# Delta rule on one core: both heads of a pair taken through the doublings step by step, and the next pair prepared ahead of the recurrence

## The chip, the core and the metric

The kernel runs on one core of a Trainium2 chip. Its engines are TensorE (PE, matrix products and the weight loads before them, PEld), VectorE (DVE), ScalarE (ACT), GpSimd (POOL) and SyncE (SP, which issues most transfers). The metric is the device time of one execution in microseconds, as the median of several runs. Lower is better.

## What is computed

Two small networks follow each other on a sequence of 512 tokens with 1024 channels, all in float32. The first block mixes tokens with a gated delta rule (4 heads of 128) beside a retention layer (4 heads of 128), then has an MLP; the second has two layers with attention and an MLP each. The change lies in the mixer of the first block. Its delta rule works on chunks; the kernel takes chunks of 128 tokens, four for each head, where the reference has 64.

```python
    kb = kc * betac[..., None]
    m = jnp.where(strict, jnp.einsum('nbhik,nbhjk->nbhij', kb, kc) * decay, 0.0)
    t_mat = lax.linalg.triangular_solve(eye + m, jnp.broadcast_to(eye, m.shape),
                                        left_side=True, lower=True, unit_diagonal=True)
    u_base = jnp.einsum('nbhij,nbhjv->nbhiv', t_mat, vb)
    w_mat = jnp.einsum('nbhij,nbhjk->nbhik', t_mat, kb * jnp.exp(gcum)[..., None])
...
    def step(state, inp):
        u_b, w_c, qk_c, qd_c, kd_c, cd_c = inp
        u = u_b - jnp.einsum('bhck,bhkv->bhcv', w_c, state)
        o = jnp.einsum('bhck,bhkv->bhcv', qd_c, state) + jnp.einsum('bhij,bhjv->bhiv', qk_c, u)
        state = state * cd_c[..., None, None] + jnp.einsum('bhck,bhcv->bhkv', kd_c, u)
        return state, o
```

## The kernel before

Activations lie with channels on the 128 partitions and the 512 tokens along the free side. Every projection is made of split products: `mm3` adds three products (high weight with high input, high with low, low with high part) to one PSUM tile `ps_pj`, and a projection of 1024 channels is eight such triples, 24 products. Three `ps_pj` tiles exist and five other PSUM tiles (pool `pw`). Weights come in blocks of 1 MB through SP's queue in the order of `_plan`, and ACT (`hi`, L252) and DVE (`lo`, L253) split each block before use.

The mixer treats the delta heads in two pairs (heads 0 and 1, heads 2 and 3), in these stages:

- `gdn_proj` projects keys, queries and values and applies the short convolution.
- `stage_a(hh)` prepares one head: keys and queries are transposed (`ps_kt`), ACT sums their squares (L602), DVE turns them into reciprocal roots (`col_rsqrt`, L425 to L435: a chain of small operations) and `brk`, `kdc`; `brk` is spread over the partitions on PE (`ps_bc`), then come the decay (`ps_gr`, `E`), the gram products (`ps_gram`, giving `N` and `QE`), `kd` (L652) and `vb`. `N` goes to DRAM (`d1`).
- `stage_b1(hp)` inverts the 16x16 diagonal blocks of the pair's triangular matrices on DVE (L678, L680) and sends them through DRAM to `cmp`.
- `stage_b2(hp)` lays them out as `T` and its transpose `U` (POOL, L696) and doubles the size of the inverted blocks three times. Each doubling has a product `ps_X` from `N` and `T`, its evacuation to `X` (DVE L721, ACT L744, ACT L764) and products `ps_T` and `ps_U`, which go back into `T` and `U`. The first doubling works on 128x64 pieces, the second on 32x32 blocks of the array, the third on 64x64 blocks. In each doubling head 0 goes through all its steps, then head 1.
- `stage_c(hp)` is the recurrence over the four chunks: for each chunk and head `ps_ks`, `vb` (DVE), `ps_u`, `u` (ACT, L790), `ps_S`, the state `S` (DVE) and `ps_o`.

Beside these stand projections of the retention heads (`rot_proj`, `ret_v`), their attention (`ret_attn`) and the gates (`gate`, with `finish`, which transposes the outputs and splits them into `mix`). Then `out_proj` applies the output weights.

A scheduler sets the order on each engine from the order of the code, dependencies and its own estimate of durations, and it fills PE's waits with products of projections. Three things in the code steer it: `in_order(i1, i2)` puts i2 behind i1, `early(prio)` gives a stretch an earlier priority, and the order of the calls at the end of `mixer`:

```python
        with early(p0):
            stage_b2(0, None, M_["rk1"])
            stage_c(0)
        with early(p1):
            stage_a(2)
            stage_a(3)
```

Only the first X product of a pair is bound to a place among the projections (`after_pe`).

Of the kernel before, what the change touches and what calls it, by code (L numbers as in the profile page):

```python
# [35 lines left out]

V_ATTN, V_MLP, V_FIN, V_MIX, V_MLP2, V_FIN2, V_GDNW, V_SUBLN, V_CONV = 0, 8, 16, 24, 40, 56, 64, 65, 66
# [20 lines left out]
def _plan():  # L58
# [6 lines left out]
    for c0, perm in ((2568, True), (2056, True), (3080, False), (1536, False), (3592, False)):  # L65
        out += [_w_cols("w_in", 0, c0 + hp * 256, perm) for hp in range(2)]
# [104 lines left out]
def build(nc, tc, a, out, phases=("mix", "mlp1", "A", "mlpA", "B", "mlpB")):  # L171
# [232 lines left out]
    def project(pieces, x, n=T, cols=P):  # L404
# [5 lines left out]
        for k in range(nk):  # L410
            hi, lo = pieces[k // KD]
            M_["pe"] = mm3(ps, (hi[:, k % KD, 0:cols], lo[:, k % KD, 0:cols]), x[k], k == 0, k == nk - 1)
# [52 lines left out]
    def out_proj(nk, x, scale_row, on_tile, reload=None, on_half=None):  # L465


        for m in range(KD):
# [20 lines left out]
            ps = project(pieces, x)  # L489
# [10 lines left out]
    def mixer(st):  # L500
# [88 lines left out]
        HD = [dict() for _ in range(4)]  # L589

        def stage_a(hh):
            H = HD[hh]
            kT, KQ, vT = H["kT"], H["KQ"], H["vT"]

            ssq = sp.tile([P, 8], F32, tag="ssq", name="ssq")
            for o, src in ((0, kT), (4, KQ[:, 1, :])):
# [6 lines left out]
                if o == 0:  # L603
                    ps_k = ps
# [7 lines left out]
            V.tensor_tensor(out=kdc, in0=rk, in1=GT["dkd"][:, :, hh], op=ALU.mult)  # L612

# [25 lines left out]
            for c2 in range(2):  # L639
# [6 lines left out]
                for aa, (o_, m_) in enumerate(((N, E2), (QE, E))):  # L646
# [4 lines left out]
            t = unit("L", NL, "kd")  # L651
            V.tensor_tensor(out=t.rearrange("p (c d) -> p c d", c=4), in0=ps_k.rearrange("p (c d) -> p c d", c=4),  # L652
                            in1=kdc.unsqueeze(2).to_broadcast([P, 4, P]), op=ALU.mult)
            H["kd"] = t
# [34 lines left out]
        def stage_b2(hp, after_g, after_pe):  # L689
# [19 lines left out]

            for i in range(2):  # L710
                H = HD[2 * hp + i]
                N, Tt, U = H["N"], H["T"], H["U"]
                X = unit("X", 2, "X")
                G.memset(X, 0.0)
# [6 lines left out]
                V.tensor_tensor(out=cols_of(X, 0).rearrange("p (c b) s -> p c b s", c=4),  # L721
                                in0=blocks(psx).rearrange("p (c b) s -> p c b s", c=4),
                                in1=cols_of(lm16, 0).unsqueeze(1).to_broadcast([P, 4, 4, 16]), op=ALU.mult)
                pst = pwt("ps_T", [P, 256])
                for c in range(4):
                    cs = slice(c * P, (c + 1) * P)
                    mm(blocks(pst[:, c * 64:c * 64 + 64]), U[:, cs], cols_of(X[:, cs], 0))
                V.tensor_tensor(out=cols_of(Tt, 0), in0=blocks(pst), in1=cols_of(Tt, 0), op=ALU.add)
                psu = pwt("ps_U", [P, 256])
                for c in range(4):  # L730
                    cs = slice(c * P, (c + 1) * P)
                    mm(blocks(psu[:, c * 64:c * 64 + 64]), X[:, cs], cols_of(U[:, cs], 1))
                V.tensor_tensor(out=cols_of(U, 1), in0=blocks(psu), in1=cols_of(U, 1), op=ALU.add)

            for i in range(2):
                H = HD[2 * hp + i]
                N, Tt, U = (H[k].rearrange("p (c i) -> p c i", c=4) for k in ("N", "T", "U"))
                ev, od = [slice(64 * b, 64 * b + 32) for b in range(2)], [slice(64 * b + 32, 64 * b + 64) for b in range(2)]
                psx = pwt("ps_X", [P, P])
                X = unit("X", 2, "X")[:, 0:P]  # L740
                for b in range(2):
                    for c in range(4):
                        mm(psx[od[b], c * 32:c * 32 + 32], N[ev[b], c, od[b]], Tt[ev[b], c, ev[b]])
                    act(out=X[od[b], :], in_=psx[od[b], :], func=AF.Copy)  # L744
                pst = pwt("ps_T", [P, P])
                psu = pwt("ps_U", [P, P])
                for b in range(2):
                    for c in range(4):
                        cs = slice(c * 32, c * 32 + 32)
                        mm(pst[od[b], cs], U[od[b], c, od[b]], X[od[b], cs])  # L750
                        mm(psu[ev[b], cs], X[od[b], cs], U[od[b], c, od[b]])
# [891 lines left out]
```

## Time and profile before

| | us |
|---|---|
| median of 3 runs | 1917.7 |
| lowest and highest run | 1908.59, 1922.01 |
| the profiled execution | 1922.43 |
| its span, first to last instruction | 1920.6 |

The profile is one execution. PE's share of busy time is high throughout, so what is worth reading is the granted clock (part 2 of the page, row PEclk), the few waits of PE, and the stretch of the mixer, which lasts from about 20 to 350 us of the span. The costliest groups of the page are the split products:

```profile
L189 PE MATMUL ps_pj<-xh,hi 128*128 128x512 f32 x1504 | 595.3, 396 | 2.1 <-ACT hi L277 2.1
```

A row of such a group has line, engine, operation, output and inputs, shape and count, then busy time, mean nanoseconds of one, and the idle time before them with what ended it. A product here is recorded with its length from issue to the last result; its cost is the distance between the starts of two neighbours. An ordinary float32 product is recorded as two instructions, so four products give eight records.

### The profile page before, as it was taken

The page shows a single profiled execution, that of the slowest core. Times are in us where ns is not written, and L with a number is a line of the kernel's source. Part 1 is how long each engine was busy: PE and PEld are TensorE (multiplying, and loading weights), DVE is VectorE, ACT ScalarE, POOL GpSimd, SP SyncE. Part 2 cuts the span into 40 slices and gives each one's busy share as a digit, 9 for nine tenths or more (in the row PEclk, how much of TensorE's full clock was granted, in tenths as well). Part 3 has the DMA queues.
Part 4 walks back from the last instruction along what each step waited for, and adds up shares of the span by engine and source line. Part 5 has one row for each costly group of instructions (what it writes and reads, how often), then busy time and mean ns, then how long its engine had stood idle before and what let it go on. Part 6 is the DMA issues. An engine that isn't in the chain of part 4 may idle for free.

```text
span 1920.6 us, 23573 instructions
## 1 busy us (share of the span) xinstructions
PE 1892.9 (99%) x9235; PEld 1554.4 (81%) x9235; DVE 1109.8 (58%) x2115; ACT 766.3 (40%) x1356; POOL 141.0 (7%) x133
## 2 busy tenths in 40 slices
PE   8999999999999999999999999999999999999998
PEld 6887777788888888877888888888888888888887
DVE  7795747666446676558543344447877754334433
ACT  5523324344234354345433134336656543213322
POOL 0231210011001103000000000001111000000000
PEclk9998989999999999999999999999999999999999
DMA  5231103222232234122323222333222232222321
GB/s 191 79 116 56 68 29 115 100 88 94 83 111 109 69 122 149 67 77 91 113 88 110 88 102 96 108 129 141 95 73 100 78 115 88 92 105 88 110 88 44
DMA packets 40271, 185.55 MB, mean 97 GB/s; under 512 B 9231, under 2 KB 11279, under 8 KB 22624
## 3 DMA queue, kind: packets, MB, share of 16 engines
q1 hardware_dynamic: 38416, 178.43, 26.5%
q0 software_dynamic: 1744, 5.61, 0.9%
q8 instruction: 73, 1.20, 0.2%
q14 instruction: 38, 0.31, 0.0%
HBM read 176.31 MB, written 7.71 MB: 96 GB/s over the span
## 4 chain that ended last, share of the span: by engine, by line
PE 55%; DVE 3%; ACT 1%; issue 1%; DVEq 0%; ACTq 0%
PE ps_pj L189 49%; PE ps_ob L189 1%; PE ps_lgb L189 1%; PE ps_po L189 1%; PE ps_aT L1421 1%; ACT junk L1438 0%; PE ps_lg L189 0%; PE ps_bc L189 0%; DVE KL L1378 0%; DVE lo L253 0%; PE ps_obT L1450 0%; PE ps_mean L189 0%; DVE nb L433 0%; PE ps_pT L1174 0%; DVE ob L1442 0%
## 5 line engine op out<-in xcount | busy, mean ns | idle before, releaser
L189 PE MATMUL ps_pj<-xh,hi 128*128 128x512 f32 x1504 | 595.3, 396 | 2.1 <-ACT hi L277 2.1
L189 PE MATMUL ps_pj<-xl,hi 128*128 128x512 f32 x1504 | 593.6, 395 | 0.0
L189 PE MATMUL ps_pj<-xh,lo 128*128 128x512 f32 x1504 | 592.8, 394 | 0.3 <-DVE lo L253 0.3
L252 ACT ACTIVATE hi<-raw 128x1024 fp32r<-128x1024 f32 (+2 forms) x306 | 315.1, 1030 | 631.3 <-PE ps_pj L189 602.1
L253 DVE TENSOR_TENSOR lo<-raw,hi 128x1024 fp32r<-128x1024 f32 (+2 forms) x306 | 367.9, 1204 | 296.2 <-ACT hi L252 293.7
L189 PEld LDWEIGHTS ps_pj<-xh,hi 128*128 128x128 f32 x1504 | 284.5, 189 | 61.9 <-ACT hi L277 3.3
L189 PEld LDWEIGHTS ps_pj<-xh,lo 128*128 128x128 f32 x1504 | 284.3, 189 | 59.0 <-DVE lo L253 1.1
L189 PEld LDWEIGHTS ps_pj<-xl,hi 128*128 128x128 f32 x1504 | 284.5, 189 | 56.9 <-DVE xl L281 0.7
L189 PE MATMUL ps_pj<-ah,lo 128*128 128x512 f32 (+1 forms) x704 | 271.0, 385 | 0.0
L189 PE MATMUL ps_pj<-al,hi 128*128 128x512 f32 (+1 forms) x704 | 270.7, 385 | 0.2 <-DVE al L278 0.2
L189 PE MATMUL ps_pj<-ah,hi 128*128 128x512 f32 (+1 forms) x704 | 270.9, 385 | 0.0
L189 PEld LDWEIGHTS ps_pj<-al,hi 128*128 128x128 f32 x704 | 132.3, 188 | 26.6 <-DVE al L278 0.5
L189 PEld LDWEIGHTS ps_pj<-ah,hi 128*128 128x128 f32 x704 | 132.3, 188 | 26.5 <-ACT ah L277 0.4
L189 PEld LDWEIGHTS ps_pj<-ah,lo 128*128 128x128 f32 x704 | 132.3, 188 | 26.1
L494 DVE TENSOR_TENSOR ot<-ps_pj,r 128x512 f32<-128x512 f32 x31 | 21.4, 692 | 108.1 <-PE ps_pj L189 108.1
L189 PE MATMUL ps_pj<-mh,hi 128*128 128x512 f32 x192 | 74.8, 394 | 1.0 <-ACT mh L277 0.9
L277 ACT ACTIVATE ah<-ms 128x512 fp32r<-128x512 f32 x64 | 40.4, 632 | 87.7 <-DVE ms L999 86.0
L189 PE MATMUL ps_pj<-ml,hi 128*128 128x512 f32 x192 | 74.4, 392 | 0.6 <-DVE ml L278 0.6
L189 PE MATMUL ps_pj<-mh,lo 128*128 128x512 f32 x192 | 74.0, 390 | 0.0
L278 DVE TENSOR_TENSOR al<-ms,ah 128x512 fp32r<-128x512 f32 x64 | 44.3, 692 | 45.3 <-ACT ah L277 45.3
L972 DVE SCALAR_TENSOR_TENSOR my<-ms,cols,my 128x511 f32<-128x511 f32 (+1 forms) x88 | 65.6, 748 | 2.8 <-ACT my L970 1.3
L1405 ACT ACTIVATE Lb<-Lb,bmn 128x512 f32<-128x512 f32 x64 | 45.6, 713 | 13.9 <-DVE bmn L1403 11.6
(343 smaller groups left out, 1907.0 us busy)
## 6 DMA issues: line engine op xcount, KB each, us to landing
raw<-w_all SPq DMA_DIRECT2D x137, 1024.0 KB
bt<-biasd SPq DMA_DIRECT2D x16, 448.0 KB
raw<-w_all SPq DMA_DIRECT2D x8, 768.0 KB
raw<-w_all SPq DMA_DIRECT2D x8, 640.0 KB
hscr<-h POOLq DMA_DIRECT2D x16, 256.0 KB, 2.4
hold<-hscr SPq DMA_DIRECT2D x16, 256.0 KB
hs<-x_t SPq DMA_DIRECT2D x8, 256.0 KB
hold<-x_t SPq DMA_DIRECT2D x8, 256.0 KB
```

The costliest lines, as they stand in the source:

```text
L189: return nc.tensor.matmul(o, lhsT=l, rhs=r, start=start, stop=stop)
L252: act(out=hv, in_=iv, func=AF.Copy)
L253: i_lo = V.tensor_tensor(out=lv, in0=iv, in1=hv.bitcast(F32), op=ALU.subtract)
L277: act(out=dst_hi, in_=src, func=AF.Copy)
L278: V.tensor_tensor(out=dst_lo, in0=src, in1=dst_hi.bitcast(F32), op=ALU.subtract)
L494: V.tensor_tensor(out=t, in0=ps, in1=scale_row, op=ALU.mult)
L972: V.scalar_tensor_tensor(out=y[:, jj:], in0=s[:, :T - jj], scalar=col(base + m), in1=y[:, jj:], op0=ALU.mult, op1=ALU.add)
L1405: act(out=L, in_=L, func=AF.Exp, scale=-1.0, bias=mn[:, j, t:t + 1], accum_out=ss[:, j, t:t + 1])
L1421: nc.tensor.transpose(ps[:, t * P:(t + 1) * P], A[t][:, kt * P:(kt + 1) * P], ident)
```

## The change

In `stage_b2` every step of a doubling is now done for both heads before the next step begins. The first product of each of the six steps of a pair (X, T, X, T, X, U) is collected in `steps`, and the last of each three split products in `units`; at the end of the mixer each step is bound behind a unit, the first behind unit 170 for pair 0 and 226 for pair 1, and each next step two units (six products) later.

`stage_a` is cut in two. The new `stage_a0` has the transposes, the squared sums, the reciprocal roots and `kd`, which ACT now copies out of PSUM before DVE scales it in place; it is called for heads 2 and 3 between `stage_b2(0)` and `stage_c(0)`. The gates of the retention heads come before those of the delta heads, with their weight blocks in the same order, and `out_proj` of the mixer sums the retention tiles (4 to 7) first.

```diff
+STEPS_0, STEPS_1 = 170, 226
...
-        return mm(ps, wl_, xh_, False, last)
+        units.append(mm(ps, wl_, xh_, False, last))
+        return units[-1]
...
+        def stage_a0(hh):
+
             H = HD[hh]
-            kT, KQ, vT = H["kT"], H["KQ"], H["vT"]
-
+            kT, KQ = H["kT"], H["KQ"]
+            kd = H["kd"] = unit("L", NL, "kd")
...
                 if o == 0:
-                    ps_k = ps
+                    act(out=kd, in_=ps, func=AF.Copy)
...
+            kv_ = kd.rearrange("p (c d) -> p c d", c=4)
+            V.tensor_tensor(out=kv_, in0=kv_, in1=kdc.unsqueeze(2).to_broadcast([P, 4, P]), op=ALU.mult)
+            H["rk"], H["brk"] = rk, brk
...
+            def step(first):
+                steps[hp].append(first)
...
                 for c in range(4):
                     cs = slice(c * P, (c + 1) * P)
                     xi = mm(blocks(psx[:, c * 64:c * 64 + 64]), N[:, cs], cols_of(Tt[:, cs], 0))
                     if i == 0 and c == 0:
+                        step(xi)
                         in_order(after_pe, xi)
...
+            for i in range(2):
+                H = HD[2 * hp + i]
+                Tt, U = H["T"], H["U"]
                 pst = pwt("ps_T", [P, 256])
...
+                for c in range(4):
+                    cs = slice(c * P, (c + 1) * P)
+                    mm(blocks(psu[:, c * 64:c * 64 + 64]), X[i][:, cs], cols_of(U[:, cs], 1))
+                V.tensor_tensor(out=cols_of(Tt, 0), in0=blocks(pst), in1=cols_of(Tt, 0), op=ALU.add)
...
         with early(p0):
             stage_b2(0, None, M_["rk1"])
+            stage_a0(2)
+            stage_a0(3)
             stage_c(0)
...
+        gate(lambda hh, gt: finish(4 + hh, R[hh]["o"], gt))
         gate(lambda hh, gt: finish(hh, HD[hh]["o"], gt))
-        gate(lambda hh, gt: finish(4 + hh, R[hh]["o"], gt))
+
+        for hp, n0 in ((0, STEPS_0), (1, STEPS_1)):
+            for j, first in enumerate(steps[hp]):
+                in_order(units[n0 + 2 * j], first)
...
+                     order=[4, 5, 6, 7, 0, 1, 2, 3] if ph == "mix" else None)
```

On PE, the second doubling of pair 0 (32x32 blocks; `ps_pj` rows are the products of projections). Before:

```order
L189 MATMUL ps_U<-U,X 128x64 x4
L189 MATMUL ps_X<-T,N 32x32 x4
L189 MATMUL ps_pj<-xl_215,hi 128x512
L189 MATMUL ps_pj<-xh_214,lo 128x512
L189 MATMUL ps_X<-T,N 32x32 x4
L189 MATMUL ps_T<-X,U 32x32
L189 MATMUL ps_U<-U,X 32x32
```

and now:

```order
L192 MATMUL ps_pj<-xh_214,lo 128x512
L192 MATMUL ps_X<-T,N 32x32 x8
L192 MATMUL ps_pj<-xh_224,hi 128x512
L192 MATMUL ps_pj<-xl_225,hi 128x512
L192 MATMUL ps_X<-T,N 32x32 x8
L192 MATMUL ps_pj<-xh_224,lo 128x512
L192 MATMUL ps_pj<-xh_138,hi 128x512
L192 MATMUL ps_pj<-xl_139,hi 128x512
L192 MATMUL ps_pj<-xh_138,lo 128x512
L192 MATMUL ps_T<-X,U 32x32
L192 MATMUL ps_U<-U,X 32x32
```

Before, T and U of one half of head 0 followed its X directly, and the other head's X came between them later; now both heads' X come first, with two and then four products behind them, and T and U of both heads follow together.

On ACT, from the last X of pair 0 (64x256) into the recurrence of pair 0, whose evacuations are the `u` rows. Before:

```order
L764 ACTIVATE X<-ps_X 64x256 x2
L790 ACTIVATE u<-ps_u 128x128
L805 ACTIVATE junk,oss<-ps_o 128x128
L790 ACTIVATE u<-ps_u 128x128
L805 ACTIVATE junk,oss<-ps_o 128x128
L790 ACTIVATE u<-ps_u 128x128
```

and now:

```order
L795 ACTIVATE X<-ps_X 64x256 x2
L611 ACTIVATE junk,ssq<-ps_kt 128x128 x4
L613 ACTIVATE kd<-ps_kt 128x512
L611 ACTIVATE junk,ssq<-ps_kt 128x128
L826 ACTIVATE u<-ps_u 128x128
L611 ACTIVATE junk,ssq<-ps_kt 128x128 x5
L826 ACTIVATE u<-ps_u 128x128
L611 ACTIVATE junk,ssq<-ps_kt 128x128
L258 ACTIVATE hi<-raw 128x1024
L611 ACTIVATE junk,ssq<-ps_kt 128x128
L613 ACTIVATE kd<-ps_kt 128x512
```

The squared sums (`junk,ssq`) and `kd` copies of heads 2 and 3 now stand among the first `u` rows, where none stood; before, the sums stood behind the last `u`.

On PE, the end of the first recurrence and the spreading of `brk` of head 2 (`ps_bc`). Before, the last rows of the recurrence were

```order
L189 MATMUL ps_u<-vb,U 128x128
L189 MATMUL ps_o<-S,qd 128x128
L599 MATMUL ps_kt<-ident,kT 128x128 x4
L599 MATMUL ps_kt<-ident,KQ 128x128 x4
L189 MATMUL ps_o<-u,QE 128x128
L189 MATMUL ps_pj<-xh_204,hi 128x512
```

and 29 more products stood between these and `ps_bc`. Now:

```order
L192 MATMUL ps_u<-vb,U 128x128
L192 MATMUL ps_o<-S,qd 128x128
L192 MATMUL ps_bc<-ident,brk 128x128 x4
L192 MATMUL ps_gr<-cg,g 128x128 x4
L192 MATMUL ps_gram<-KQ,kT 128x256 x4
L669 MATMUL ps_vt<-ident,vT 128x128 x4
L192 MATMUL ps_o<-u,QE 128x128
L192 MATMUL ps_pj<-xl_205,hi 128x512
```

The transposes have left this place, and `ps_bc` to `ps_vt` of head 2 stand ahead of the recurrence's last product.

More of the change, by code (lines that the diff above doesn't have):

```diff
@@ L401, in build, with project @@
             norm_sq(st0, k, hs0[k], after=xh_act[min(k + 3, KD - 1)])
-    def project(pieces, x, n=T, cols=P):
+    def project(pieces, x, n=T, cols=P, order=None):
         if pre:
@@ L409, in project @@
         nk = len(x)
-        for k in range(nk):
+        order = order or list(range(nk))
+        for k in order:
             hi, lo = pieces[k // KD]
-            M_["pe"] = mm3(ps, (hi[:, k % KD, 0:cols], lo[:, k % KD, 0:cols]), x[k], k == 0, k == nk - 1)
+            M_["pe"] = mm3(ps, (hi[:, k % KD, 0:cols], lo[:, k % KD, 0:cols]), x[k], k == order[0], k == order[-1])
         return ps
@@ L462, in token_major, with out_proj @@
         act(out=dst, in_=ps, func=AF.Copy)
-    def out_proj(nk, x, scale_row, on_tile, reload=None, on_half=None):
+    def out_proj(nk, x, scale_row, on_tile, reload=None, on_half=None, order=None):
         for m in range(KD):
@@ L488, in out_proj @@
                 continue
-            ps = project(pieces, x)
+            ps = project(pieces, x, order=order)
             if scale_row is None:
@@ L650, in stage_a @@
             nc.sync.dma_start(d1[hh], N.rearrange("p (c i) -> p c i", c=4))
[L651 to L654, printed above, removed]
             ps = pwt("ps_vt")
@@ L719, in stage_b2 @@
                     if i == 0 and c == 0:
+                        step(xi)
                         in_order(after_pe, xi)
-                V.tensor_tensor(out=cols_of(X, 0).rearrange("p (c b) s -> p c b s", c=4),
+                V.tensor_tensor(out=cols_of(X[i], 0).rearrange("p (c b) s -> p c b s", c=4),
                                 in0=blocks(psx).rearrange("p (c b) s -> p c b s", c=4),
                                 in1=cols_of(lm16, 0).unsqueeze(1).to_broadcast([P, 4, 4, 16]), op=ALU.mult)
+            for i in range(2):
+                H = HD[2 * hp + i]
+                Tt, U = H["T"], H["U"]
                 pst = pwt("ps_T", [P, 256])
[L725 to L728, printed above, removed]
                 psu = pwt("ps_U", [P, 256])
@@ L749, in stage_b2 @@
                         cs = slice(c * 32, c * 32 + 32)
-                        mm(pst[od[b], cs], U[od[b], c, od[b]], X[od[b], cs])
-                        mm(psu[ev[b], cs], X[od[b], cs], U[od[b], c, od[b]])
+                        ti = mm(pst[od[b], cs], U[od[b], c, od[b]], X[i][od[b], cs])
+                        mm(psu[ev[b], cs], X[i][od[b], cs], U[od[b], c, od[b]])
+                        if i == b == c == 0:
+                            step(ti)
                 for b in range(2):
@@ L758, in stage_b2 @@
                 H = HD[2 * hp + i]
-                N, Tt, U = (H[k].rearrange("p (c i) -> p c i", c=4) for k in ("N", "T", "U"))
+                N, Tt = (H[k].rearrange("p (c i) -> p c i", c=4) for k in ("N", "T"))
                 psx = pwt("ps_X", [P, 256])
                 for c in range(4):
-                    mm(psx[hi_, c * 64:c * 64 + 64], N[lo_, c, hi_], Tt[lo_, c, lo_])
-                X = unit("X", 2, "X")[:, 0:256]
-                act(out=X[hi_, :], in_=psx[hi_, :], func=AF.Copy)
+                    xi = mm(psx[hi_, c * 64:c * 64 + 64], N[lo_, c, hi_], Tt[lo_, c, lo_])
+                    if i == c == 0:
+                        step(xi)
+                X[i] = unit("X", 2, "X")[:, 0:256]
+                act(out=X[i][hi_, :], in_=psx[hi_, :], func=AF.Copy)
+            for i in range(2):
+                H = HD[2 * hp + i]
+                U = H["U"].rearrange("p (c i) -> p c i", c=4)
                 psu = pwt("ps_U", [P, 256])
                 for c in range(4):
-                    mm(psu[lo_, c * 64:c * 64 + 64], X[hi_, c * 64:c * 64 + 64], U[hi_, c, hi_])
+                    ui = mm(psu[lo_, c * 64:c * 64 + 64], X[i][hi_, c * 64:c * 64 + 64], U[hi_, c, hi_])
+                    if i == c == 0:
+                        step(ui)
                 V.tensor_copy(U[lo_, :, hi_], psu[lo_, :].rearrange("p (c j) -> p c j", c=4))
@@ L927, in mixer @@
         gdn_proj(0, "v")
-        stage_a(0)
-        stage_a(1)
+        for hh in range(2):
+            stage_a0(hh)
+            stage_a(hh)
         gdn_proj(1, "kq")
```

36 lines of the change are left out of this document (24 added, 12 removed).

## The prediction, written before the changed kernel ran

> **What bounds the kernel now.** I read the page first, parts 1 and 2.
>
> ```profile
> span 1920.6 us, 23573 instructions
> PE 1892.9 (99%) x9235; PEld 1554.4 (81%) x9235; DVE 1109.8 (58%) x2115; ACT 766.3 (40%) x1356; POOL 141.0 (7%) x133
> PEclk9998989999999999999999999999999999999999
> ```
>
> TensorE (PE) is busy for 99% of the span, so time is won only where PE waits or where its work runs slowly. The clock row dips below full speed three times, all early, and the last two dips lie in the delta rule. So I read the window view there (each row: the window, its length, busy time and count of PE, weight load, DVE, ACT and POOL, the granted clock, DMA) and then the waits of PE between 140 and 352 us.
>
> ```profile
> 154.30:157.70 3.40, 3.20 (x82) 2.21 (x81) 1.38 (x5) 1.64 (x4) 0.00 (x0) 1.00 0.02 5
> 157.70:171.40 13.70, 13.70 (x71) 10.01 (x70) 4.16 (x10) 1.90 (x7) 0.00 (x0) 0.50 0.00 0
> 191.90:195.30 3.40, 1.05 (x7) 0.62 (x7) 2.60 (x13) 0.00 (x0) 1.04 (x1) 1.00 0.00 0
> 195.30:198.70 3.40, 3.40 (x16) 3.22 (x16) 1.42 (x4) 0.00 (x0) 0.00 (x0) 0.50 0.02 5
> 253.30:256.70 3.40, 3.20 (x70) 2.57 (x69) 0.85 (x3) 0.54 (x2) 0.00 (x0) 1.00 0.00 0
> 256.70:273.80 17.10, 17.10 (x104) 12.36 (x103) 5.23 (x14) 3.27 (x9) 0.00 (x0) 0.50 0.18 62
> 297.70:301.10 3.40, 2.71 (x19) 2.19 (x20) 2.70 (x5) 1.15 (x2) 1.04 (x1) 1.00 0.02 5
> 888.20:891.60 3.40, 1.87 (x10) 1.15 (x9) 3.40 (x7) 1.96 (x4) 0.00 (x0) 1.00 0.00 0
> PE ps_bc L189 <- DVE brk L610: 2.4, 1, 2.4
> PE ps_oT L914 <- POOL o L820: 1.2, 2, 0.7
> PE ps_X L189 <- POOL T L696: 0.7, 1, 0.7
> PE ps_T L189 <- ACT X L744: 0.4, 2, 0.2
> ```
>
> The clock is exactly half in three stretches of 13.7, 3.4 and 17.1 us, which are 4, 1 and 5 times 3.4: it is granted in windows of about 3.4 us. Each half-speed stretch follows a window poor in work. In 191.9 to 195.3 PE idled for 2.4 us. In 154.3 to 157.7 and 253.3 to 256.7 it was busy for 3.20 of 3.40 us, but almost all its 82 and 70 instructions are the 32x32 and 64x64 blocks of the doublings. In 888.2 to 891.6 PE was busy for only 1.87 us, with 10 instructions of full size, and the clock stayed at 1.00. So the gate weighs how much of the array works, not how long PE counts as busy. The half-speed stretches are the cost: 34.2 us in which work takes twice its time.
>
> ```profile
> 153.48 0.43 PE L189 MATMUL ps_X<-T,N 32*32 32x32 f32 x8
> 153.84 0.50 PE L189 MATMUL ps_pj<-xl,hi 128*128 128x512 f32 x1
> 154.18 0.40 PE L189 MATMUL ps_pj<-xh,lo 128*128 128x512 f32 x1
> 157.36 0.82 PE L189 MATMUL ps_X<-T,N 64*64 64x64 f32 x8
> 158.12 0.79 PE L189 MATMUL ps_pj<-xh,hi 128*128 128x512 f32 x1
> 158.71 0.63 PE L189 MATMUL ps_pj<-xl,hi 128*128 128x512 f32 x1
> 159.14 0.63 PE L189 MATMUL ps_pj<-xh,lo 128*128 128x512 f32 x1
> 163.61 1.11 PE L189 MATMUL ps_X<-T,N 64*64 64x64 f32 x8
> 164.65 0.79 PE L189 MATMUL ps_pj<-xl,hi 128*128 128x512 f32 x1
> 191.71 0.39 PE L189 MATMUL ps_pj<-xl,hi 128*128 128x512 f32 x1
> 191.94 0.39 PE L189 MATMUL ps_pj<-xh,lo 128*128 128x512 f32 x1
> ```
>
> These are rows of PE's timeline (start, duration). From start to start a product of a projection (ps_pj) takes 191.94 - 191.71 = 0.23 us at full clock and 159.14 - 158.71 = 0.43 at half. Eight records of a 64x64 step take 164.65 - 163.61 = 1.04 us at half clock.
>
> The same two closing windows once more, counting the products of projections alone, and the last transposes and the row for 888.2 in which the clock held:
>
> ```profile
> 154.30:157.70 3.40, 1.50 (x5) 0.48 (x3) 0.23 (x1) 0.00 (x0) 1.00 0.02 5
> 253.30:256.70 3.40, 0.75 (x3) 0.31 (x3) 0.00 (x0) 0.00 (x0) 1.00 0.00 0
> 297.70:301.10 3.40, 1.18 (x4) 0.68 (x4) 0.00 (x0) 0.00 (x0) 1.00 0.02 5
> 888.84 0.60 PE L1144 MATMUL ps_v<-ident,v 128*128 128x128 f32 x4
> ```
>
> Of the five products in 154.3 to 157.7 two had begun before it (153.84 and 154.18), so three fill it; three also in 253.3 to 256.7. In 888.2 to 891.6 four of the ten instructions are transposes (ps_v) and six are products, one or two of which only reach in.
>
> **The change, part by part.** First, the doublings. Both heads now do each step before the next begins, and the next may start only six products later. Between the first X step and the last U step of a pair stand, by the order of PE's instructions, 30 products instead of 25, and they are spread evenly. The work on PE is the same, so what changes is which window holds what. The poorest stretch is now the 32x32 one: X of head 0, two products, X of head 1, four products, then 64 records of T and U. With the rows above it lasts about 0.4 + 0.7 + 0.4 + 1.0 + 1.3 = 3.8 us (X as at 153.48, products as above, the 1.3 from the rows below). So any 3.4 us of it hold nearly six products, 6 x 0.23 = 1.4 us of full-array work, where both closing windows had three. The nearest row on the open side is 888.2 to 891.6: four to six products and four transposes of 128 columns. Six products lie on the open side, with little room. I take both stretches as gone.
>
> ```profile
> 155.29 0.21 PE L189 MATMUL ps_T<-X,U 32*32 32x32 f32 x1 [0.20 <-ACT X L744]
> 155.75 0.50 PE L189 MATMUL ps_pj<-xh,hi 128*128 128x512 f32 x1
> ```
>
> Between these two starts, 0.46 us apart, stand 22 records of 32x32 blocks: 21 ns each, 1.3 us for 64.
>
> The gain is half of 13.7 + 17.1 = 30.8 us, that is 15.4. Small blocks may not halve: the eight records at 157.36 took 158.12 - 157.36 = 0.76 us, half of it at half clock, which gives 0.60 at full, where half of 1.04 is 0.52. Seven such groups lie in the two stretches: 7 x 0.08 = 0.6 lost. The bounds of this term are 0, if both stages stay cold, and 15.4. [...]
>
> The 0.4 us on X (L744) go, since two products and the other head's step now stand between a step and its evacuation. The 0.7 on POOL's T go: before, the second pair's X came right behind the T blocks of POOL; now 64 products (14.6 us) stand behind the last retention product. What is late next there is nothing I can see.
>
> Second, the preparation. stage_a0 for heads 2 and 3 (16 transposes, 16 squared sums, two chains of small DVE operations, kd) stands ahead of stage_c(0). brk is then ready when the recurrence ends. The 2.4 us wait goes, and with it its cold window of 3.4 us, worth 1.7. But these operations now stand in the queues that the recurrence uses. On ACT each u that PE waits for (L790) stands behind them:
>
> ```profile
> 186.33 0.28 ACT L602 ACTIVATE junk<-ps_kt 128x128 f32<-128x128 f32 x1
> 186.73 0.28 ACT L602 ACTIVATE junk<-ps_kt 128x128 f32<-128x128 f32 x1
> 218.78 2.03 ACT L462 ACTIVATE Vr<-ps_tm 128x512 f32<-128x512 f32 x4
> 193.19 0.17 DVE L433 SCALAR_TENSOR_TENSOR nb<-rkq 128x8 f32<-128x8 f32 x1
> 193.39 0.17 DVE L434 TENSOR_TENSOR nb<-nb,nx 128x8 f32<-128x8 f32 x1
> L652 DVE TENSOR_TENSOR kd<-ps_kt,kdc 128x512 f32<-128x512 f32 x2 | 1.4, 681 | 0.0
> ```
>
> A squared sum costs 186.73 - 186.33 = 0.40 us of ACT, and 16 cost 6.4; the new copy of kd is nearest to the Vr copy, 2.03/4 = 0.51, twice 1.0. So 7.4 us of ACT enter the recurrence. On DVE enter two chains of 15 small operations at 193.39 - 193.19 = 0.20 and two kd at 0.68, 7.4 us, among the S and vb that PE waits for. The cover is 22 more products in that recurrence (56 instead of 34), 22 x 0.23 = 5.1 us. I charge 7.4 - 5.1 = 2.3 us of new waits; the ends are 0, if all is covered, and 14.8, if ACT and DVE delay PE in turn. For heads 0 and 1 the kd copy runs beside projections and costs nothing; its cover is the 60% of the span in which ACT is idle, and without it the price would be 1.0 us. After the recurrence the second head's gram products wait for the first head's decay, with 16 products between instead of 41: the chain from the first gr through E, POOL and N to the next KQ fits about 7 us of PE work, and I charge 0.
>
> Third, the ends. The retention heads' gates now come first, with their weights loaded in that order: equal blocks on SP's queue, cost 0. The 1.2 us that the last transposes wait for POOL's o stay: the chain from the last o through the reciprocal root to POOL is as long as before; bounds -1.2 and +1.4 (seven small operations at 0.20 that may come to stand ahead). The output projection takes the retention tiles first; same products, 0.
>
> Sum: -15.4 + 0.6 - 0.4 - 0.7 - 2.4 - 1.7 + 2.3 = -17.7 us. The profiled execution took 1922.4 us (its span of 1920.6 and 1.8 around it), so the sum gives 1904.7. The median of the runs is 1917.7, 4.7 lower. If those 4.7 lie in work that the change leaves alone, the changed kernel's median is 1900.0; if they are cold windows that the median run did not have, it is 1904.7. I take 1902, a gain of 0.8%.
>
> **The rivals.** (a) The gate still closes in a doublings stage, so the change does not do what it is for. For it speak the 32x32 stretch (nearly six products, where the gate's bound lies somewhere between three and six) and any wait in it; against it the row at 888.2. One stage cold returns about 7.5 us: 1910. Both return 15: 1917.
>
> (b) Slower than before: the recurrence becomes a chain of ACT and DVE. For it speaks that ACT and DVE run in the order of their queues: the evacuation of an X block started at 157.65, with no idle time before it, right behind a weight copy of 1.06 us.
>
> ```profile
> 156.57 1.06 ACT L252 ACTIVATE hi<-raw 128x1024 fp32r<-128x1024 f32 x1 [0.42 <-PE ps_pj L189]
> 157.65 0.27 ACT L744 ACTIVATE X<-ps_X 32x128 f32<-32x128 f32 x1
> ```
>
> Its full price is 14.8 instead of 2.3, and if these waits empty the windows of the recurrence, five of them at half clock add 8.5: 1902 + 12.5 + 8.5 = 1923. It decides from 17.7 us of new delay on; the 22 further products speak against it.
>
> (c) Transposes do not hold the clock open. The 16 new ones stand in a row behind the 64x64 blocks, with nearly no products for 2.8 us, so a window would close there and one or two cold ones follow, 1.7 us each: 1905. Against it speaks 297.7 to 301.1: 19 instructions, four of them products and the rest transposes, and the clock stayed at 1.00. [...]
>
> **How the numbers follow.** My case has 0.72, with its own range 1896 to 1908 (0 to 6 us of new waits, and either reading of the median); (a) has 0.10 for one stage and 0.06 for both; (b) 0.06; (c) 0.06. The range 1895 to 1911 holds my case, (c) and one cold stage: 0.88 less tails, a little over 0.8. About 1% is what a measurement of this kernel can tell from no change, here below 1898.5 or above 1936.9. A third of my case lies below 1898.5, which gives 0.24 for faster; nothing but an extreme of (b) lies above 1936.9, 0.03; same has 0.73.
>
> **What would show it.** Right: the clock at 1.00 through both doublings stages and after the recurrence; no wait on brk; no wait on POOL's T; small new waits of PE on u and vb in the first recurrence, 1 to 4 us in sum. Wrong: half clock in a window that follows the 32x32 blocks (a), or the transposes (c); PE idle for over 10 us in the recurrence (b). A total outside 1895 to 1911 with all of these right would mean that time moved outside the mixer, where I expect none.

## The result and the profile after

The changed kernel takes 1902.47 us (median of 10 runs, 1900.9 to 1904.8). The kernel before, run beside it, takes 1916.15 us (median of 10, 1908.59 to 1922.79). The ratio of the two is 0.9932, with a 95% interval of 0.9911 to 0.9952: a gain of 0.7%. The forecast was 1902, with "same" (within 1%) as the likeliest. The profiled execution took 1903.76 us; the one of before took 1922.43.

Parts 1 and 2 of the page of the changed kernel:

```profile
span 1901.9 us, 23565 instructions
PE 1876.8 (99%) x9235; PEld 1544.8 (81%) x9235; DVE 1107.0 (58%) x2115; ACT 767.2 (40%) x1360; POOL 143.3 (8%) x133
PEclk9999999999999999999999999999999999999999
```

PE's count of instructions is the same, and its busy time is 16.1 us shorter: the same work ran faster. The span is 18.7 us shorter. The two dips of the clock row that lay in the delta rule are gone. (The prediction speaks of three dips in the row of before; the row shows two.)

The next two fences have one row of the window view for each kernel, from the first X step of pair 0 to the first broadcast behind the mixer (the columns are those of the prediction's windows). The kernel before:

```profile
145.40:356.10 210.70, 205.67 (x1226) 165.15 (x1224) 127.76 (x373) 72.39 (x187) 27.80 (x27) 0.92 0.22 73
```

The changed one:

```profile
144.80:336.20 191.40, 188.74 (x1226) 154.27 (x1224) 125.63 (x373) 71.89 (x189) 29.94 (x27) 1.00 0.24 81
```

This stretch alone gained 19.3 us. PE's busy time fell by 205.67 - 188.74 = 16.9 us, and its idle time from 210.70 - 205.67 = 5.0 to 191.40 - 188.74 = 2.7 us. The clock went from 0.92 to 1.00.

Single windows of the changed kernel: the 32x32 steps of pair 1, and a place far behind the mixer:

```profile
243.80:247.20 3.40, 3.40 (x80) 2.50 (x82) 1.01 (x1) 2.01 (x5) 0.00 (x0) 1.00 0.00 0
868.40:871.80 3.40, 1.88 (x10) 1.15 (x9) 3.40 (x7) 2.06 (x4) 0.00 (x0) 1.00 0.00 0
871.80:875.20 3.40, 3.40 (x16) 2.38 (x17) 3.40 (x7) 2.44 (x4) 0.00 (x0) 0.50 0.00 0
```

And the first of them with the products of projections alone:

```profile
243.80:247.20 3.40, 1.93 (x6) 0.97 (x6) 0.00 (x0) 0.00 (x0) 1.00 0.00 0
```

The poorest window with 32x32 blocks (243.80) holds 80 records, of which six are products, and the clock stays open (1.00 from 247.2 to 250.6). The last two rows of the longer fence are a surprise: the window at 868.40 has the same content as the one at 888.2 of the kernel before (1.88 us busy with 10 instructions, against 1.87 with 10), on which the clock had stayed open. Here the next window runs at half clock.

The waits of PE between 100 and 400 us in the changed kernel:

```profile
PE ps_tm L468 <- DVE QE L663: 1.3, 1, 1.3
PE ps_oT L950 <- POOL o L856: 0.7, 1, 0.7
PE ps_gram L192 <- DVE KQ L631: 0.4, 2, 0.3
```

The waits on brk, on POOL's T and on ACT's X are gone. None on u or vb has come. Two new ones stand behind the first recurrence: the transposes of Vr wait for DVE's QE, and the gram products for KQ.

### The profile page after: what moved, and what is told of

It reads as the page before. It is cut to its first block, busy times and chain, and to the rows that moved or that the text cites. A ratio compares the mean times of both kernels' runs of the same rounds, so it can differ in the third digit from the quotient of the medians.

```text
span 1901.9 us, 23565 instructions
## 1 busy us (share of the span) xinstructions
PE 1876.8 (99%) x9235; PEld 1544.8 (81%) x9235; DVE 1107.0 (58%) x2115; ACT 767.2 (40%) x1360; POOL 143.3 (8%) x133
## 2 busy tenths in 40 slices
DMA packets 40271, 185.55 MB, mean 98 GB/s; under 512 B 9231, under 2 KB 11279, under 8 KB 22624
## 4 chain that ended last, share of the span: by engine, by line
PE 56%; DVE 3%; ACT 1%; issue 1%; DVEq 0%; ACTq 0%
PE ps_pj L192 50%; PE ps_ob L192 1%; PE ps_lgb L192 1%; PE ps_po L192 1%; PE ps_aT L1464 1%; ACT junk L1481 0%; PE ps_lg L192 0%; DVE lo L259 0%; PE ps_bc L192 0%; DVE KL L1421 0%; DVE nb L440 0%; PE ps_obT L1493 0%; PE ps_pT L1217 0%; PE ps_mean L192 0%; DVE nb L441 0%
```

## The experiments

The theory: a window of about 3.4 us (the half-clock stretches of before last 13.7, 3.4 and 17.1 us) with little work of the whole array closes the gate, and the change keeps all windows of the doublings above that bound; the preparation takes waits away. The main rivals: the preparation alone carries the gain; doing both heads together carries it, whatever stands between the steps; the profiled runs were lucky in the phase of the windows. All times are medians of at least six runs. The ratios are to the kernel before, whose own runs spread over 17 us, so that the narrower kernels are better compared by their medians and extremes:

| kernel | median us | lowest to highest | mean clock | ratio, 95% interval |
|---|---|---|---|---|
| before, again | 1916.8 | 1907.1 to 1924.2 | 0.987 to 0.997 | 1.0003 [0.9975, 1.0031] |
| changed, again | 1902.6 | 1900.3 to 1904.8 | 0.996 to 0.998 | 0.9949 [0.9931, 0.9966] |
| doublings alone | 1912.8 | 1905.3 to 1917.4 | 0.989 to 0.997 | 0.9989 [0.9965, 1.0014] |
| doublings alone, bound | 1906.3 | 1904.3 to 1911.4 | 0.993 to 0.997 | 0.9949 [0.9928, 0.9970] |
| preparation alone | 1909.9 | 1907.8 to 1917.5 | 0.989 to 0.995 | 0.9986 [0.9959, 1.0012] |
| steps not held apart | 1922.3 | 1916.7 to 1924.3 | 0.987 to 0.991 | 1.0041 [1.0018, 1.0065] |
| three products between | 1907.5 | 1903.0 to 1911.1 | 0.992 to 0.997 | 0.9973 [0.9958, 0.9988] |
| nine products between | 1907.7 | 1906.1 to 1908.5 | 0.995 to 0.996 | 0.9960 [0.9943, 0.9978] |
| before, with filler | 1915.7 | 1912.5 to 1916.5 | 0.995 to 0.998 | 1.0003 [0.9988, 1.0019] |
| order of the ends as before | 1903.9 | 1902.6 to 1907.0 | 0.995 to 0.998 | 0.9945 [0.9921, 0.9970] |
| changed, filler at the start | 1899.6 | 1899.1 to 1900.4 | 0.997 to 0.998 | 0.9935 [0.9920, 0.9950] |
| the same, Vr held back | 1899.8 | 1899.2 to 1901.5 | 0.997 to 0.999 | 0.9921 [0.9895, 0.9947] |

**Both kernels once more.** No edit.

> The kernel before, unchanged, to see what spreads its runs (1908.6 to 1922.8 us). Theory (the clock's windows run free of the program, so a run closes more or fewer of them in the two doublings stages): the mean granted clock differs from run to run between about 0.987 and 0.994 and the time with it, about 1.7 us for each window of 3.4 us at half clock; times 1908 to 1923, median about 1915. Rival (the spread is noise of the transfers or of other origin): the clock is the same 0.987 in all runs while the time spreads.

> The changed kernel, unchanged, on the same chip as the three beside it. Theory (six products between steps hold the clock open whatever the phase of its windows): all runs at a mean clock of 0.995 to 0.998, 1900 to 1906 us, median 1902.5. Rival (the changed kernel was lucky in its phase): some runs at 0.987 to 0.993 and 1909 to 1920 us.

Measured: before spreads as the theory says, and its clock with it: 1907.1 us at 0.997, 1924.2 at 0.987. One of these twelve runs, 1919.5 at 0.990, lies between the groups that follow. Beside the experiments ran 84 more runs of the kernel before. They fall into three groups: 38 runs of 1907.1 to 1911.8 us (0.995 to 0.998), 22 of 1913.6 to 1917.7 (0.991 to 0.993) and 24 of 1921.1 to 1924.5 (0.987 to 0.989). The means, 1909.3, 1915.4 and 1923.0, lie 6.1 and 7.6 us apart, near the 7.5 us that the prediction worked out for one doublings stage. Both profiles of before are of the third group, with both stages at half clock. That a run of the first group has both open, and one of the second group one, is inferred from clock and time; no profile shows it. The changed kernel stayed at 0.996 or more in all 16 runs: it was not lucky. The means of the outer groups lie 13.7 us apart, all with one kernel. That the windows do not move with the program shows in the profiles of the two kernels, whose work is the same at the start: the products of the first mean begin at 20.97 us in before and at 21.12 in the changed kernel, 0.15 later, and the half clock behind that wait begins at 21.2 and at 21.9, 0.7 later.

**The preparation alone.** The doublings are those of the kernel before:

```diff
-            X = [None, None]
-            for i in range(2):
...
+            for i in range(2):
+                H = HD[2 * hp + i]
+                N, Tt, U = H["N"], H["T"], H["U"]
...
-        for hp, n0 in ((0, STEPS_0), (1, STEPS_1)):
-            for j, first in enumerate(steps[hp]):
-                in_order(units[n0 + 2 * j], first)
```

> The changed kernel with the doublings of the kernel before (one head after the other, steps not held apart); the preparation stays ahead. Theory: half clock in one or both doublings stages again, no wait on brk: 1909 to 1916 us, 3 to 5 us below the kernel before in its own runs. Rival (the preparation carries the gain): 1902 to 1905.

Measured: 1909.9 us, with more half clock than the changed kernel in every run (0.995 at most). Two windows of its profile, the first in pair 0 with the stretch that it closed, the second in pair 1:

```profile
153.10:156.50 3.40, 3.20 (x81) 2.33 (x74) 1.87 (x6) 1.92 (x5) 0.00 (x0) 1.00 0.02 5
156.50:166.70 10.20, 10.20 (x57) 7.09 (x57) 3.09 (x7) 0.98 (x4) 0.00 (x0) 0.50 0.00 1
241.80:245.20 3.40, 3.20 (x68) 2.47 (x66) 1.21 (x4) 0.76 (x3) 0.00 (x0) 1.00 0.00 0
```

Both windows are busy for 3.20 of 3.40 us, both with small blocks and about four products; one closed the gate and the other did not. Counting products does not tell the two apart: they take 1.46 us in the window that closed and 1.13 in the one that held, which has some of the 128x64 blocks of the first doubling besides. So the bound lies near such windows, and the doublings of before stood near it. The preparation does not open the clock there; this rival falls.

**The doublings alone.** The preparation goes back behind the recurrence:

```diff
             stage_b2(0, None, M_["rk1"])
-            stage_a0(2)
-            stage_a0(3)
             stage_c(0)
         with early(p1):
-            stage_a(2)
-            stage_a(3)
+            for hh in (2, 3):
+                stage_a0(hh)
+                stage_a(hh)
```

> The changed kernel with the preparation of heads 2 and 3 put back behind the first recurrence; the doublings stay as changed, with their steps six products apart. Theory (the doublings carry the gain, through the clock): clock 1.00 in both doublings stages, the wait on brk of about 2.4 us and one window at half clock behind it (1.7) are back, the 1.7 us of new waits are gone: 1903 to 1907 us. Rival (the preparation carries the gain): as slow as before, 1912 to 1918.

A miss: 1912.8 us. The second doublings stage was still at half clock:

```profile
238.00:241.40 3.40, 2.71 (x24) 2.71 (x25) 0.85 (x2) 0.00 (x0) 1.86 (x2) 1.00 0.00 0
241.40:261.90 20.50, 20.50 (x154) 15.22 (x154) 4.79 (x12) 2.78 (x7) 0.00 (x0) 0.50 0.14 52
```

The window that closes holds 24 records of the first steps (128x64) and no product, and PE stands idle in it for 0.7 us, waiting for POOL's T. The places of the steps are counted in products from the kernel's start. Here the preparation stands later and the X of pair 1 came past its place, so that T and U followed it at once. That is a fault of the edit, and it shows that the rule on the steps works only where its numbers fit the order. With the second count moved from 226 to 229 the gaps are back:

```diff
-STEPS_0, STEPS_1 = 170, 226
+STEPS_0, STEPS_1 = 170, 229
```

> The first doublings-alone kernel with the second pair's steps bound from unit 229 on, so that its X stands behind 30 products and six products stand between all of its steps (in the first one two of these gaps were empty). Theory: clock 1.00 in both doublings stages in all runs; what is left against the whole change are the wait on brk and a window at half clock behind it: median 1904 to 1907 us, spread under 5 us. Rival (the preparation is needed for the clock to stay open): a doublings stage still closes in many runs, median 1910 to 1915.

Measured: 1906.3 us, ten of twelve runs from 1904.3 to 1907.9, as the theory said. Two ran at 0.993 and 1911, which it had not allowed for. The profile is of one of these two:

```profile
237.40:240.80 3.40, 1.85 (x12) 1.25 (x10) 0.58 (x2) 0.00 (x0) 3.40 (x4) 1.00 0.01 2
240.80:254.40 13.60, 13.58 (x52) 12.33 (x52) 3.26 (x6) 1.06 (x1) 1.18 (x1) 0.50 0.21 77
```

and its wait there (total, times, longest):

```profile
PE ps_X L192 <- POOL T L708: 1.6, 2, 1.3
```

The X of pair 1 waits 1.6 us for POOL's T, and the window with this wait closes the gate. In the whole change 64 products stand ahead of that X, and the wait is gone. So the early preparation does more than take the wait on brk away: with it this wait ahead of the second doublings stage is gone too.

**Steps not held apart.** Both heads still do each step together, but nothing holds a step back:

```diff
-        for hp, n0 in ((0, STEPS_0), (1, STEPS_1)):
-            for j, first in enumerate(steps[hp]):
-                in_order(units[n0 + 2 * j], first)
```

> The changed kernel without the rule that holds a step back until six products after the step ahead; both heads still do each step together. The order then has only 3 products among the 32x32 steps (X, T, U of both heads, 96 records). Theory (what counts is the products that each window holds): the gate closes in both doublings stages, half clock for 10 to 20 us in each run: 1909 to 1917 us. Rival (doing both heads together is enough, since it takes away the waits between the steps): 1902 to 1905.

Measured: 1922.3 us, worse than expected and worse than before, with a mean clock of 0.991 at most. A window in pair 0, the stretch behind it, and the window's products alone:

```profile
151.50:154.90 3.40, 3.34 (x99) 2.62 (x99) 1.13 (x4) 0.97 (x5) 0.00 (x0) 1.00 0.19 74
154.90:161.80 6.90, 6.90 (x39) 5.42 (x39) 2.00 (x7) 1.54 (x7) 0.00 (x0) 0.51 0.00 0
151.50:154.90 3.40, 0.97 (x3) 0.43 (x3) 0.00 (x0) 0.00 (x0) 1.00 0.19 74
```

PE is busy for 3.34 of 3.40 us, with no wait worth the name, and the gate closes: three products and 96 small records are too little. Pair 1 closed in another way. The wait of PE there, and the window that holds most of it:

```profile
PE ps_T L192 <- DVE X L738: 2.6, 1, 2.6
233.50:236.90 3.40, 1.57 (x12) 1.35 (x11) 3.19 (x11) 0.00 (x0) 0.22 (x1) 1.00 0.00 0
```

With no products held between X and T, PE waits 2.6 us for X, and the 17 us behind this window run at half clock (0.50 from 236.9 to 254.0). So most of the half clock of this kernel follows waits, and the 6.9 us in pair 0 alone show that a full window of small blocks closes the gate. Doing the heads together without the gaps makes the windows poorer than before, by small blocks and by waits; this rival falls.

**Three and nine products between steps.**

```diff
-                in_order(units[n0 + 2 * j], first)
+                in_order(units[n0 + 1 * j], first)
```

(and 3 * j in the other).

> The changed kernel with three products between steps instead of six; nothing else. Theory (the products in a window decide): windows over the 32x32 steps hold about three or four products and the gate closes in most runs, 0.988 to 0.993, 1908 to 1919 us. Rival (a gap of any size takes the waits between steps away, and that was the gain): 1901 to 1905 us.

> The changed kernel with nine products between steps instead of six. Theory: clock open in all runs as with six, so nothing more to win, 0 to 3 us of new waits as the recurrences keep fewer products: 1901 to 1906 us. Rival (six is on the edge and some windows still close): a median 1 to 3 us below that of the changed kernel, with less spread.

Both came out near 1907.6 us, outside the ranges of their theories, and the slower time of the first does not have the cause that was written down. With three products the doublings stayed open in the profile:

```profile
152.40:155.80 3.40, 3.40 (x93) 2.47 (x90) 0.86 (x3) 1.05 (x4) 0.00 (x0) 1.00 0.13 51
152.40:155.80 3.40, 1.91 (x6) 0.97 (x6) 0.00 (x0) 0.00 (x0) 1.00 0.13 51
```

(all instructions, then the products alone). The expectation counted three or four products in such a window; there are six, since the small records go by faster than assumed. What costs time is the wait on QE behind the first recurrence and the windows that it closes. In the kernel with three products the wait is

```profile
PE ps_tm L468 <- DVE QE L663: 3.5, 1, 3.5
```

and its windows

```profile
193.40:196.80 3.40, 1.40 (x8) 0.83 (x5) 3.30 (x6) 0.93 (x2) 3.32 (x4) 1.00 0.00 0
196.80:203.60 6.80, 5.33 (x15) 4.39 (x16) 4.12 (x16) 1.39 (x2) 1.48 (x2) 0.50 0.15 43
```

In the kernel with nine, waits and then the window:

```profile
PE ps_tm L468 <- DVE QE L663: 3.3, 1, 3.3
PE ps_gram L192 <- DVE KQ L631: 1.4, 2, 1.2
```

```profile
200.50:203.90 3.40, 0.15 (x1) 0.00 (x0) 3.37 (x6) 0.00 (x0) 2.03 (x2) 1.00 0.00 0
```

In both orders 41 products stand between the last U of pair 0 and the second pair's first broadcast, where the changed kernel has 49. That does not bring PE to the wait earlier, counted from that broadcast: it gets there after 15.0 and 16.2 us, in the changed kernel after 15.2. The chain takes longer, on DVE (its rows stand further down). For three products that is 3.5 - 1.3 = 2.2 us of wait and up to 5.33/2 = 2.7 us of half clock, at most 4.9 in all; the profiled executions lie 4.2 us apart, the medians 4.9. For nine the waits are 3.3 + 1.4 against 1.3 + 0.4, 3.0 us more, and the 3.4 us behind the window ran at half clock (0.51 from 203.9 to 207.3), which is up to 1.7; the medians lie 5.1 apart. So in these profiles six products win over three and nine by what happens behind the recurrence, not by the clock in the doublings.

**Filler in the kernel before.** Three products of no use behind the X, and three behind the T and U, of each 32x32 step of a head:

```diff
+        def filler(after):
+            fp = pwt("ps_fill")
+            for j in range(3):
+                f = mm(fp, x[6][0][:, 0:P], x[7][0])
+                if j == 0:
+                    in_order(after, f)
+            return f
```

> The kernel before with 24 products of no use (three behind each 32x32 X step and three behind each 32x32 T and U step of a head; read by nothing). They cost 24 times 0.23 us = 5.5 us and take no wait away. Theory (the array work of a window decides): the doublings stay at clock 1.00, so no run near 1922: the open runs of before (1908) plus 5.5, that is 1911 to 1916 with all at a mean clock of 0.995 or more. Rival (the gate closes for another reason, as the waits of the steps): the spread of before moved up by 5.5, that is 1913 to 1930, with runs at 0.987.

Measured: 1915.7 us, 1912.5 to 1916.5, all runs at 0.995 or more; no run of the two groups with stages at half clock is left. A window over the 32x32 steps, then its products of projections, then its filler:

```profile
154.50:157.90 3.40, 3.40 (x52) 2.14 (x52) 1.15 (x4) 0.54 (x2) 0.00 (x0) 1.00 0.02 5
154.50:157.90 3.40, 0.73 (x2) 0.30 (x2) 0.00 (x0) 0.00 (x0) 1.00 0.02 5
154.50:157.90 3.40, 1.88 (x6) 0.93 (x6) 1.00 0.02 5
```

Useless work, with heads, steps and preparation as before, keeps the gate open (a clock of 1.00 from 145 to 166 us and from 245 to 265). The wait of 0.7 us on POOL's T stands as before; only the two waits on X, 0.4 us in all, went with the filler. The price of the filler is 1915.7 - 1909.3 = 6.4 us against the open runs of before (24 x 0.23 = 5.5 expected), so it wins only against the closed ones. Together with pair 0 of the kernel whose steps are not held apart, which closed without a wait, this shows that the array work of a window decides.

**The order of the ends.** Gates and output projection in the order of before:

```diff
-        gate(lambda hh, gt: finish(4 + hh, R[hh]["o"], gt))
         gate(lambda hh, gt: finish(hh, HD[hh]["o"], gt))
+        gate(lambda hh, gt: finish(4 + hh, R[hh]["o"], gt))
...
-                     order=[4, 5, 6, 7, 0, 1, 2, 3] if ph == "mix" else None)
+                     order=None)
```

> The changed kernel with the order of the gates and of the output projection's tiles as before. Theory (these swaps are worth nothing): the same as the changed kernel within 1 us, 1901.5 to 1903.5, the wait of the last transposes on POOL's o 1.2 us in place of 0.7. Rival (the swaps carry some of the gain): 1904 to 1907.

Measured: 1903.9 us, 1.3 above the changed kernel, between theory and rival; the runs of the two overlap. In the waits of PE stands a new one on the gate's product:

```profile
PE ps_oT L950 <- POOL o L856: 0.7, 2, 0.4
PE ps_pj L192 <- DVE gs L942: 0.5, 1, 0.5
```

The wait on o is the same 0.7 in both. So the swaps are worth about 1 us at most, 0.5 of it this wait. The profiled execution here, 1906.96 us, is the slowest of the nine and ran one more window at half clock (342.6 to 346.1), so the rest is within what windows do from run to run.

**A filler at the first mean, and the wait on QE.** Eight products of no use stand where PE waits 1.95 us for the first mean; the second kernel also holds the third block of Vr transposes back:

```diff
+        fp = pwt("ps_fill")
+        for j in range(8):
+            f = mm(fp, w0[0][0][:, 7, :], st0.x[7][0])
+            if j == 0:
+                in_order(M_["pe"], f)
...
+        in_order(units[207], tms[2])
```

> The changed kernel with eight products of no use (128x512, into a PSUM tile that nothing reads) in the 1.95 us in which PE waits for the first mean, at about 19 us. They add work and take no wait away. Theory (a window with little array work closes the gate): the 6.8 us at half clock behind it go, 3.4 us less, with at most 0.3 us of delay: median 1898 to 1900. Rival (that stretch at half clock has another cause): 1902 to 1903.

> The changed kernel with the eight products of no use at the first mean, and with the third block of Vr transposes held back until ten further products, which now fill the 1.3 us in which PE waits for DVE's QE after the first recurrence. Theory (that wait is of PE alone, and the products are work that is due anyway): the wait goes, 1.3 us less than with the filler alone (1899.6): 1898 to 1899. Rival (the wait moves behind: retention starts later and waits for Vr or sT): 1899 to 1900.

The filler gains 3.0 us (1902.6 to 1899.6), with the tightest spread of all. The place in the changed kernel:

```profile
18.50:21.90 3.40, 1.45 (x11) 1.02 (x10) 2.17 (x4) 3.14 (x6) 0.82 (x2) 1.00 0.67 280
21.90:28.70 6.80, 6.47 (x17) 4.68 (x17) 5.39 (x17) 1.34 (x4) 0.00 (x0) 0.50 0.40 151
```

and in the one with the filler:

```profile
18.00:21.40 3.40, 3.24 (x19) 2.54 (x19) 3.14 (x4) 3.24 (x6) 0.99 (x2) 1.00 0.68 287
21.40:28.00 6.60, 6.60 (x34) 5.46 (x34) 5.42 (x19) 1.98 (x4) 0.94 (x1) 1.00 0.62 228
```

Nearly twice the instructions run in about the same time, 34 in 6.60 us at a clock of 1.00 against 17 in 6.80 at 0.50. This version beats both kernels. Holding the Vr transposes back gained nothing (1899.8): the wait on QE went, but retention now waits for DVE in its place, as the rival said:

```profile
PE ps_ro L192 <- DVE sT L923: 1.5, 1, 1.5
```

## Why the prediction was right, step by step

**The gate weighs array work.** Shown by the filler in the kernel before (six products of no use in the window at 154.5, clock 1.00 behind it) and by the steps not held apart (PE busy for 3.34 of 3.40 us, clock 0.51 behind). The work that counts is not that of the products of projections alone (a window of the changed kernel at 148.2 had 0.18 us of one of them beside records of the 128x64 steps, PE busy for 3.40 of 3.40 us, and the clock behind it was 1.00), and the figure for the bound was taken too sharply. Windows with four products went both ways (1.46 us of them closed, 1.13 us held, both in the kernel with the preparation alone), and the row at 888.2, which the prediction took as the nearest open one, closed in the changed kernel at 868.4 with the same content (0.50 behind it). Six products beside 32x32 blocks were open in every window seen (1.93 us of them at 243.8 in the changed kernel, 1.91 at 152.4 in the one with three between steps).

**The doublings, -15.4 + 0.6.** Right. Both stages ran at full clock. With the window behind brk that is 34.2 us at half clock less, which is worth 17.1, and PE's busy time fell by 16.9 in that stretch: the allowance of 0.6 for small blocks was 0.2. Its working has a slip: of the 0.76 us at 157.36, 0.34 lie ahead of the half clock and 0.42 behind its start, which gives 0.34 + 0.42/2 = 0.55 us at full clock and not 0.60, and so an allowance of 7 x 0.03 = 0.2. One duration in the argument was too long: 64 records of 32x32 were put at 1.3 us. The first of them and the product behind the last:

```profile
156.00 0.21 PE L192 MATMUL ps_T<-X,U 32*32 32x32 f32 x1
156.87 0.50 PE L192 MATMUL ps_pj<-xh,hi 128*128 128x512 f32 x1
```

They take 0.87 us, so windows held more products than forecast, and in the profile of the kernel with three between the steps the clock held too (1.00 in the 3.40 us behind 155.8).

**The waits, -0.4, -0.7, -2.4, and the window behind brk, -1.7.** All went. Rivals (a), (b) and (c) did not happen: no window closed behind the 32x32 blocks or the 16 transposes, and PE idled for 0.2 us in the stretch that has the transposes and most of the recurrence:

```profile
162.60:184.60 22.00, 21.84 (x132) 17.67 (x132) 13.78 (x57) 12.29 (x57) 0.00 (x0) 1.00 0.14 49
```

Here 16 transposes passed at a clock of 1.00, but with products close behind, so this row speaks against rival (c) and does not measure transposes alone. A window behind the second recurrence, in the second profile of the changed kernel, says more:

```profile
271.60:275.00 3.40, 3.40 (x30) 3.19 (x29) 2.84 (x17) 1.81 (x7) 0.00 (x0) 1.00 0.49 207
```

Of its 3.40 us the transposes `ps_oT`, 22 of them, take 2.49 and two products that began ahead of it 0.38, and the clock stayed at 1.00 behind it.

**The new waits, +2.3.** The size is about right (1.3 + 0.4 = 1.7), and that is luck, since the place is not. The step that failed is the one that charged 0 for the chain from the first gr to the second KQ and QE because it "fits about 7 us of PE work". In the recurrence itself, where 2.3 was charged, ACT and DVE kept up. Behind it the chain did not: from the first gr (185.55) to the end of the second KQ (194.45 + 0.68) it took 9.6 us, and QE came 6 us later still. Rows of DVE and POOL there, in the changed kernel:

```profile
196.08 0.16 DVE L434 TENSOR_SCALAR ni<-nx 128x4 int32<-128x4 int32 x1
196.90 1.46 POOL L643 TENSOR_TENSOR E<-E,rkq 128x512 f32<-128x512 f32 x1 [1.92 <-ACT E L639]
197.35 1.03 DVE L436 TENSOR_SCALAR fc<-ni 128x4 int32<-128x4 int32 x1
198.44 1.30 POOL L646 TENSOR_TENSOR E<-E,cg 128x512 f32<-128x512 f32 x1
198.62 1.14 DVE L441 TENSOR_TENSOR nb<-nb,nx 128x4 f32<-128x4 f32 x1
199.69 0.68 DVE L901 TENSOR_TENSOR vs<-ps_pj,rs 128x512 f32<-128x512 f32 x1
200.29 0.41 DVE L663 TENSOR_TENSOR N<-ps_gram,E 128x256 f32<-128x256 f32 x1
200.62 0.41 DVE L663 TENSOR_TENSOR QE<-ps_gram,E 128x256 f32<-128x256 f32 x1
```

QE stands behind N in DVE's queue, and N reads what POOL's second operation makes (L646), which ends at 198.44 + 1.30 = 199.74. N could not start before that, so POOL's part of the chain explains most of this wait, and the order on DVE at most the 0.55 us from there to 200.29. Small operations on 128x4 elements, 0.16 us elsewhere, take 1.03 and 1.14 us here, and each ends within 0.03 us of the end of an operation of POOL; in the changed kernel they end just as N's input is ready. In the kernel with nine products between steps they cost more:

```profile
198.79 1.29 POOL L646 TENSOR_TENSOR E<-E,cg 128x512 f32<-128x512 f32 x1
201.36 1.19 DVE L441 TENSOR_TENSOR nb<-nb,nx 128x4 f32<-128x4 f32 x1
203.07 0.41 DVE L663 TENSOR_TENSOR N<-ps_gram,E 128x256 f32<-128x256 f32 x1
```

There N's input was ready at 200.08 and N started 3.0 us later, behind two small operations of 1.2 us and vs; with three products it was ready at 194.80 and N started at 197.37. So the waits of 3.3 and 3.5 us in these two kernels are longer by what small operations of DVE take beside POOL. Where the wait was moved, retention waited for sT, which stood behind a weight split of 1.68 us (`lo`) in DVE's queue.

**The ends, 0.** Between 0 and 1.3 us of gain; the wait on o became 0.7 instead of 1.2 and stayed so with the order undone.

**From the profile to the median.** The sum gave 1904.7 for the profiled execution, which took 1903.76: in the stretch above the terms make -17.7 and 19.3 were gained, most of the difference in idle time (-2.4 against -1.2). Ahead of the stretch 0.6 us were gained and behind it 1.2 lost, where the window at 871.8 ran at half clock (up to 1.7 us), which the prediction had not foreseen. For the median it left two readings, 1900.0 and 1904.7, and took a value between. The runs of before decide for the second: they differ in how many windows close, and its profiled run had both stages closed, which by clock and time is so in 24 runs of 84. So 18.7 us is the gain against the kernel before at its worst; against its mean over those 84 runs, 1914.8, it is 12.2. Against the open runs of before, 1909.3, 6.7 remain (1909.3 - 1902.6), and the other 5.5 are the clock in the doublings. Of the 6.7 the profiles show 2.4 as less idle time of PE, and 1.7 is the window behind brk, if it closes in those runs too; in the profile of before with filler, whose doublings stayed open, it did (192.1 to 195.5 at half clock). The other 2.6 are not settled, since no profile shows an open run of before. So it was partly luck that 1902 met the measured 1902.47: the right reading alone would have given 1904.7. Of the 2.2 us between, 1.0 is a gain of the profiled execution beyond the sum (18.7 against 17.7), and 1.3 that the median run of the changed kernel is faster than its profiled one.

## What to carry to other kernels

Read the granted clock beside PE's busy share: here a window in which PE was busy for 3.20 of 3.40 us, with small blocks, was followed by 13.7 us at a clock of 0.50, and the cure was to spread full-size products evenly among them (six in such a window, clock 1.00). Waits closed the gate as well (the one of 2.4 us on brk, with 3.4 us at 0.50 behind it), and there the cure was to cover or remove the wait. The runs of before spread in steps of 6.1 and 7.6 us, at mean clocks of 0.987 to 0.998, and both its profiles fell in the slowest group; for such a kernel take the mean over many runs, since one profile shows one of its groups. When work is moved ahead, follow the chain that it feeds: here the next wait was on a product of ACT, POOL and DVE in turn, and some small operations of DVE took 1.0 to 1.2 us in place of 0.16 beside POOL's.

## What was not expected of the hardware

Equal work closed the gate in one kernel and not in the other (1.88 and 1.87 us of 3.40, ten instructions each), so near the bound something that these records do not show decides, the exact place of the window among the instructions for instance (in the changed kernel the window starts about 0.1 us later among the same instructions); this stays open. Work of no use won 3.0 us where PE would have idled for 1.95 us. The time of before falls into three groups about 7 us apart, by the number of doublings stages at half clock as far as clock and time tell. Some small operations of DVE, 0.16 us elsewhere, took 1.0 to 1.2 us beside POOL's and ended with them.
